# Hybrid decoder layer: activations read channel-major only, with rstd as a row, opening transfers in halves, and unread products ahead of the first matmul

## The chip, the cores and the metric

The kernel runs as one program on one core of a Trainium2 chip. The metric is the device time of one execution in microseconds. Three runs of the kernel before gave 767.24, 767.46 and 767.67 us, so the median is 767.46 us.

## The reference, cut to what matters

The layer has three token mixers in parallel, gated and merged, and then a mixture of experts. For the change only the opening matters: two RMS norms, and the projections that read them.

```python
def rmsnorm(x, g):
    y = x * rsqrt(mean(x * x, axis=-1, keepdims=True) + EPS)
    return y * g
h = rmsnorm(x, g_mix)                  # x (512 tokens, 1024 channels); all of w_in reads h
proj = h @ w_in
kv = rmsnorm(mem, g_mem) @ w_mem_kv    # mem (256 tokens, 1024 channels); k_m and v_m of the memory branch
k_m = rmsnorm(k_m, g_km)               # per head; v_m is used as it is
```

Everything is float32. The kernel keeps that precision in its projections by splitting each operand into a high part (a cast to fp32r) and a low part (the rest), and by adding three products: high by high, high by low and low by high.

## The kernel before

The work is written in program order, and a scheduler with a timing model of its own orders each engine's queue at build time. It prefers the earlier instruction among those it takes to be ready. Every queue is then executed in order. Two groups of instructions, the taps of the convolution and the top-k, are written with a low priority and fill what the vector engine (DVE) has left.

The opening is the section "mem kv". It multiplies the transposed memory tokens with w_mem_kv in eight chunks of 128 channels (`for k in range(KD)`). A chunk of weights is 128x1024 floats, 512 KB, from `raw_w` (L132) into a ring of three tiles. `split_w` makes its high part `wh` by a cast on ScalarE (ACT, L127) and its low part `wl` by a subtraction on DVE (L128), each in a ring of three as well. `evac_split` (L153 on ACT, L154 on DVE) does the same for an activation, times a gain per channel. Each chunk has 12 matmuls of 512 columns (`mm3`, L157 to L159) into four PSUM accumulators kv00, kv01, kv10 and kv11, first both halves of the columns for the memory tokens m=0, then for m=1. Three of the four have the PSUM tag "mm", which has three buffers.

Inside the same loop h is made. x is loaded with tokens on the partitions (four tiles of 512 KB), and a sum of squares per token (`sum_sq`, L223 on ACT, L225 on DVE) goes through `rsqrt` (L145 on DVE, then a power on GpSimd, L146). The tokens are scaled on DVE into `xn` (L265). 32 matmuls against an identity transpose them (L248), and eight `evac_split` make `hh` and `hl`. The raw memory tokens (two tiles of 512 KB) are loaded token-major as well, for their own sums of squares. They take two of the three buffers of the tag "hw", which three of the h tiles use.

What follows the opening is `cm_unit` (L314): 24 matmuls of 512 columns for 128 output channels, high by high over all eight chunks of h, then low weights by high h, then high weights by low h. The first one needs a PSUM buffer of the tag "mm", that is, one of the kv accumulators has to have been read. Such units, the attention branches and the gates run until about 415 us. There the pools of the first part are closed, and `fetch` (L779) starts to stream the 192 expert chunks of 512 KB through one queue, into buffers that the first part gives back. The queue of SyncE (SP) carries nearly all loads, in order.

Of the kernel before, what the change touches and what calls it, by code (L numbers as in the profile page):

```python
# [89 lines left out]
def build(nc, tc, I, O, dbg=None):  # L90
    V, A, G, T, SY = nc.vector, nc.scalar, nc.gpsimd, nc.tensor, nc.sync
    es = ExitStack()
    with es:
# [9 lines left out]
                dbg.mark(label)  # L103


        xt0 = [mpool.tile([P, D], F32, name=f"x{t}", tag="mg", bufs=4) for t in range(NT)]
        p1a, p1b, pps = ExitStack(), ExitStack(), ExitStack()
        hp = es.enter_context(tc.tile_pool(name="hp", bufs=1, side="right"))
        bp = p1b.enter_context(tc.tile_pool(name="bp", bufs=1, side="right"))
# [9 lines left out]
        tri16 = cpool.tile([P, 2 * P], BF16, name="tri16")  # L119
        nhalf = cpool.tile([P, 16], F32, name="nhalf")  # L120
        G.memset(nhalf, -0.5)

        def small(name, n, dt=F32, tag="small", bufs=16):
            return cpool.tile([P, n], dt, name=name, tag=tag, bufs=bufs)
# [53 lines left out]
        def g2(tag, name, dt=F32, shape=(P, 512)):  # L178
            pool = bp if tag in ("A", "B") else gp
            return pool.tile(list(shape), dt, name=name, tag=tag, bufs=BUFS[tag])  # L180

        def h_pairs(name):

            hi, lo = [], []
            for k in range(KD):
                if k >= 3:
                    x2 = hp.tile([P, 1024], F32R, name=f"{name}{k}", tag="hw" if k < 6 else "hx", bufs=3 if k < 6 else 2)
                    hi.append(x2[:, 0:512])
                    lo.append(x2[:, 512:1024])
# [27 lines left out]
            V.tensor_mul(t[:, :, 3, :], sin, g1)  # L217
            return t

        def sum_sq(ss, xt, on_act, tag="ms"):  # L220
            junk = g2(tag, "junk", BF16, (P, D))
            if on_act:
                A.activation(junk, xt, AF.Square, accum_out=ss)  # L223
            else:
                V.tensor_tensor_reduce(junk, xt, xt, scale=1.0, scalar=0.0, op0=ALU.mult, op1=ALU.add, accum_out=ss)  # L225


        mark("mem kv")
        kv_raw = [raw_w("kv", 0)]
        mx = [hp.tile([P, D], F32, name=f"m{i}", tag=("hx", "hw")[i // 2], bufs=2 + i // 2) for i in range(4)]  # L230
        SY.dma_start(mx[0], I["memt"][0])
        kv_raw.append(raw_w("kv", 1))
        SY.dma_start(mx[1], I["memt"][1])
        SY.dma_start(csg[:, 0:P], I["cst"][:, C_KEEP:C_KEEP + P])
        kv_raw.append(raw_w("kv", 2))
        mh = [g2("A", f"mh{k}", F32R) for k in range(4)]
        ml = [g2("A", f"ml{k}", F32R) for k in range(4)]
        for k in range(KD):
            o = (k % 2) * 256
            evac_split(mh[k // 2][:, o:o + 256], ml[k // 2][:, o:o + 256],  # L240
                       mx[k // 4][:, (k % 4) * 256:(k % 4 + 1) * 256], Q["g_mem"][:, k:k + 1])
        hh, hl = h_pairs("h")

        def transpose_x():
            for k in range(KD):
                ps = (trt if k % 2 == 0 else sct)()
                for t in range(NT):
                    T.transpose(ps[:, t * P:(t + 1) * P], xn[2 * t + k // 4][:, (k % 4) * P:(k % 4 + 1) * P], ident)  # L248
                evac_split(hh[k], hl[k], ps, Q["g_mix"][:, k:k + 1])

        kvp = [[mmt("kv00"), mmt("kv01")], [mmt("kv10"), pvt("kv11")]]
        xn, rm = [], []
        for k in range(KD):
            if k < NT:
                SY.dma_start(xt0[k], I["x"][k])
            elif k < NT + 2:
                SY.dma_start(mx[k - 2], I["mem"][k - NT])
            if k == 3:
                for t in range(NT):
                    ss = small("ss", 1)  # L260
                    sum_sq(ss, xt0[t], t != 1, "y")
                    rsqrt(ss, ss, 1.0 / D, EPS)
                    for i in range(2):
                        xn.append(g2("B", f"xn{t}{i}"))
                        V.tensor_scalar_mul(xn[-1], xt0[t][:, i * 512:(i + 1) * 512], ss)  # L265
            if k == 5:
                transpose_x()
            wh, wl = split_w(kv_raw[k] if k < RING else raw_w("kv", k))
            for m in range(2):
                o = (k % 2) * 256 + m * P  # L270
                ah, al = mh[k // 2][:, o:o + P], ml[k // 2][:, o:o + P]
                for n in range(2):
                    mm3(kvp[m][n], ah, al, wh[:, n * 512:(n + 1) * 512], wl[:, n * 512:(n + 1) * 512],
                        k == 0, k == KD - 1)
        SY.dma_start(sm[:, 2 * KD:], I["sm"][:, 2 * KD:])
        V.tensor_mul(gqk, Q["g_qm"], Q["g_km"])
        for m in range(2):
            rm.append(small("rm", 1, tag="rm", bufs=2))
            sum_sq(rm[m], mx[2 + m], True)
            rsqrt(rm[m], rm[m], 1.0 / D, EPS)  # L280
        vmh, vml, kn = [], [], []
        for m in range(2):
# [508 lines left out]
        def eat(tag, name, bufs=1, dt=F32):  # L791
            return ea.tile([P, 1024], dt, name=name, tag=tag, bufs=bufs)

        x_v = I["xt"].rearrange("k p n -> p k n")
        X = []
        for c in range(KD // 2):
            xt = rp.tile([P, 2, S], F32, name=f"xr{c}", tag="xc", bufs=2)
            SY.dma_start(xt, x_v[:, 2 * c:2 * c + 2])
            X.append(xt)
        wo_raw = [raw_w("wo", c) for c in range(KD)]  # L800
        gB = eat("wg", "gB")
# [504 lines left out]
def layout(x, mem, g_mix, w_in, b_gate, g_qa, g_ka, g_idx_k, conv_w, conv_b, ln_g, ln_b, g_mem, w_mem_kv,  # L1306
# [45 lines left out]
    def row(a):  # L1352
# [8 lines left out]
                 g_ffn=col(g_ffn, KD), b_r=np.concatenate([row(b_rg), row(b_re)], axis=1), w_r=wr, pad=np.zeros((P, 1), np.float32))  # L1361
    sm = np.ascontiguousarray(np.concatenate([parts[k] for k in S_OFF], axis=1).astype(np.float32))
    x, mem = f(x)[0], f(mem)[0]
    return dict(x=x.reshape(NT, P, D), xt=np.ascontiguousarray(x.T).reshape(KD, P, S), mem=mem.reshape(2, P, D),
                memt=np.ascontiguousarray(mem.T.reshape(2, 4, P, 256).transpose(0, 2, 1, 3)).reshape(2, P, D), wp=wp, we=we, sm=sm,
                gf=f(g_ffn), cst=constants())

# [34 lines left out]
```

## Time and profile before

| what | value |
|---|---|
| median of 3 runs | 767.46 us |
| profiled execution | 766.1 us |
| its span, first to last instruction | 764.2 us |
| mean granted TensorE clock | 0.991 |
| TensorE (PE) busy | 717.2 us, 94% |
| DVE busy | 477.5 us, 62% |
| ACT busy | 266.3 us, 35% |
| GpSimd (POOL) busy | 90.8 us, 12% |

The span is 1.9 us shorter than the profiled execution; the rest lies before the first and after the last instruction. Times in the trace count from the first instruction. PE is matmul, PEld the loading of its weights. A row of the timeline gives the start, the length, the engine, the line and what is written and read, and, in brackets, how long the engine had stood idle and what ended that. Matmuls are pipelined, so the distance between two starts tells more than the length of one. DMA share is the busy share of the core's 16 DMA engines.

### The profile page before, as it was taken

To read this page: it belongs to the slowest core of one execution; us is meant where nothing else is said; L and a number is where in the kernel's file an instruction comes from. 1 tells how busy PE (TensorE), PEld (TensorE's weight loads), DVE (VectorE), ACT (ScalarE), POOL (GpSimd) and SP (SyncE) were. 2 spreads that over 40 slices of the span, in tenths; PEclk is the share of its full clock that TensorE was granted. 3 is DMA by queue.
4 is the path that set the end of the run, shared out by engine and by line. 5 is a ranking of instruction groups with operands and counts; after the bars stand their busy time and mean duration, and the time that the engine had idled before them with its cause. 6 is when DMAs were issued, how large, how long until landed. Compare 5 with 4: busy or idle time off the path is not lost. (4 is left out here: it accounts for less than half of the span.)

```text
span 764.2 us, 10080 instructions
## 1 busy us (share of the span) xinstructions
PE 717.2 (94%) x3468; PEld 477.9 (63%) x3468; DVE 477.5 (62%) x1085; ACT 266.3 (35%) x503; POOL 90.8 (12%) x82
## 2 busy tenths in 40 slices
PE   6999999999999999999998999989999998889882
PEld 5778888887878778888776888834333333233220
DVE  5879989999999999999986844272112112111100
ACT  6722254455633376237775422101111111000100
POOL 1110010011000050000000000021226322100010
PEclk9999999999999999999999999999999999999997
DMA  9632221213222222321214799999999999999982
GB/s 357 232 121 82 88 79 55 82 58 111 83 83 83 83 84 72 98 80 55 84 55 150 273 378 340 329 315 377 400 378 359 354 370 387 361 381 395 391 324 49
DMA packets 56684, 161.13 MB, mean 211 GB/s; under 512 B 9508, under 2 KB 17956, under 8 KB 56624
## 3 DMA queue, kind: packets, MB, share of 16 engines
q1 hardware_dynamic: 42320, 147.74, 52.2%
q0 software_dynamic: 6624, 8.46, 4.8%
q10 hardware_dynamic: 7680, 4.20, 1.9%
q8 instruction: 29, 0.48, 0.2%
q14 instruction: 31, 0.25, 0.1%
HBM read 162.93 MB, written 13.11 MB: 230 GB/s over the span
## 5 line engine op out<-in xcount | busy, mean ns | idle before, releaser
L1165 PE MATMUL up<-we,xt 128*64 128x512 f32 x544 | 140.8, 599 | 5.4 <-DMA we<-in_we 5.4
L127 ACT CAST wh<-w 128x1024 fp32r<-128x1024 f32 (+2 forms) x75 | 78.3, 1046 | 80.4 <-PE proj L314 22.2
L128 DVE TENSOR_TENSOR wl<-w,wh 128x1024 fp32r<-128x1024 f32 (+2 forms) x75 | 90.9, 1213 | 13.0 <-ACT wh L127 11.2
L1165 PEld LDWEIGHTS up<-we,xt 128*64 128x64 f32 x544 | 39.1, 136 | 77.5 <-issue 59.1
L328 DVE SCALAR_TENSOR_TENSOR y<-u,conv_wh,y 128x512 f32<-128x512 f32 x120 | 84.2, 745 | 0.3
L1155 DVE COPY y<-dn 128x512 f32<-128x512 f32 x17 | 11.8, 692 | 108.9 <-PE dn L1179 108.9
L1179 PE MATMUL dn<-we,acth 128*64 128x512 f32 x272 | 73.5, 596 | 0.6 <-issue 0.6
L314 PE MATMUL gate<-h,wh 128*128 128x512 f32 x240 | 67.9, 397 | 0.0
L1154 ACT COPY y<-dn 128x512 f32<-128x512 f32 x17 | 10.0, 586 | 123.7 <-PE dn L1179 72.7
L1179 PEld LDWEIGHTS dn<-we,acth 128*64 128x64 f32 x272 | 24.0, 137 | 44.9 <-issue 36.3
L314 PEld LDWEIGHTS gate<-h,wh 128*128 128x128 f32 x240 | 44.4, 188 | 9.5
L1156 POOL DMA_INDIRECT out<-y,midx x16 | 25.4, 1585 | 147.5 <-DVE y L1155 106.5
L314 PE MATMUL gate<-h,wl 128*128 128x512 f32 x120 | 34.7, 399 | 0.0
L314 PE MATMUL mm<-h,wh 128*128 128x512 f32 x120 | 32.7, 397 | 0.0
L422 ACT ACTIVATE gt<-gate,bgate 128x512 f32<-128x512 f32 x24 | 16.5, 686 | 39.8 <-PE gate L314 39.5
L1138 ACT COPY xt<-xtr 128x512 f32<-128x512 f32 x18 | 10.4, 585 | 56.4 <-PE xtr L1137 52.4
L1173 DVE COPY acth<-atr 128x256 f32<-128x256 f32 x17 | 7.2, 425 | 36.0 <-PE atr L1171 28.4
L1148 DVE SCALAR_TENSOR_TENSOR acts<-up,mwt,acts 128x256 f32<-128x256 f32 x16 | 7.7, 484 | 32.3 <-ACT acts L1147 29.6
L604 DVE MAX8 v<-score 128x8 f32<-128x256 f32 (+2 forms) x48 | 26.6, 557 | 0.8
L605 DVE MATCH_REPLACE8 score<-v,score 128x256 f32<-128x256 f32 (+2 forms) x48 | 26.0, 542 | 0.0
L314 PEld LDWEIGHTS gate<-h,wl 128*128 128x128 f32 x120 | 22.4, 188 | 5.4 <-issue 0.5
L314 PEld LDWEIGHTS mm<-h,wh 128*128 128x128 f32 x120 | 22.4, 188 | 5.1
(400 smaller groups left out, 1442.0 us busy)
## 6 DMA issues: line engine op xcount, KB each, us to landing
we<-in_we SPq DMA_DIRECT2D x192, 512.0 KB
w<-in_wp SPq DMA_DIRECT2D x75, 512.0 KB
x<-in_x SPq DMA_DIRECT2D x4, 512.0 KB
xr<-in_xt SPq DMA_DIRECT2D x4, 512.0 KB
out<-x1t ACTq DMA_DIRECT2D x8, 256.0 KB
h2d<-x1t ACTq DMA_DIRECT2D x6, 256.0 KB
m<-in_memt SPq DMA_DIRECT2D x2, 512.0 KB
m<-in_mem SPq DMA_DIRECT2D x2, 512.0 KB
```

Of the source, the lines that this page charges most:

```text
L127: A.copy(wh, w)
L128: V.tensor_sub(wl, w, wh.bitcast(F32))
L314: T.matmul(ps, a[:, k * P:(k + 1) * P], b[k], start=(a is wh and b is rh and k == 0), stop=(b is rl and k == n - 1))
L328: V.scalar_tensor_tensor(Y[c], U[c][:, j:j + S], w, Y[c], op0=ALU.mult, op1=ALU.add)
L422: A.activation(t, ps, AF.Tanh, scale=0.5, bias=bgate[:, b * 8 + c:b * 8 + c + 1])
L604: V.max(v8, sel[t])
L605: V.match_replace(sel[t], v8, sel[t], GONE)
L1138: (A.copy if i or j == 0 else V.tensor_copy)(xt[i], ps.bitcast(F32))
L1155: V.tensor_copy(y[:, 512:1024], yp[1])
L1156: G.indirect_dma_start(out=O["out"], out_offset=bass.IndirectOffsetOnAxis(ap=ix[:, col:col + 1], axis=0), in_=y, in_offset=None, bounds_ch ...
L1165: T.matmul(ps[h * CAP:(h + 1) * CAP], xt[k // 4][:, o + h * CAP:o + (h + 1) * CAP], ws[h][:, i * 512:(i + 1) * 512], start=(k == 0), stop= ...
L1179: T.matmul(yp[n][h * CAP:(h + 1) * CAP], at[:, f * P + h * CAP:f * P + (h + 1) * CAP], ws[h][:, n * 512:(n + 1) * 512], start=(f == 0), st ...
```

## The change

- x is loaded only channel-major (`xt`, laid out by the host as four tiles of two chunks each), early in the opening. The token-major x, its sums of squares per token, the scaling into `xn` and the 32 transposes are gone.
- Squares are taken per channel on ACT, added up over the eight chunks in two accumulators, one on DVE and one on POOL. Eight matmuls against a column of ones sum over the channels (`rstd_x`), and `rsqrt` gives rstd. Four matmuls against the identity spread it as a row over all partitions (`norm_x`). Each chunk of x is multiplied by that row, even chunks on DVE (from PSUM), odd ones on POOL (from a copy in SBUF), and split into `hh` and `hl` by `evac_split`, now out of SBUF.
- Small copies out of `wl` of chunks 4 and 6 (`late`), overwritten at once, keep `rstd_x` and `norm_x` behind those splits.
- The first weight chunk and the first tile of memory tokens are loaded and the weights split in halves. Eight matmuls of 128 columns on a tile of ones, whose result nobody reads, stand ahead of the first real one.
- In each kv chunk the order of the four accumulators is by columns first, then by tokens. The raw memory tokens are loaded after the eight chunks, in four pieces, into the tag "B".

```diff
+        warm = cpool.tile([P, P], F32, name="warm")
+        V.memset(warm, 1.0)
...
+        junk = trt()
+        for _ in range(8):
+            T.matmul(junk[:, 0:P], warm, warm, start=True, stop=True)
+        w0 = wpool.tile([P, 1024], F32, name="w", tag="w")
+        mx = [hp.tile([P, D], F32, name=f"m{i}", tag="hx", bufs=2) for i in range(2)]
+        for i in range(2):
+            SY.dma_start(w0[:, i * 512:(i + 1) * 512], I["wp"][W_KEYS.index(("kv", 0)), :, i * 512:(i + 1) * 512])
+            SY.dma_start(mx[0][:, i * 512:(i + 1) * 512], I["memt"][0, :, i * 512:(i + 1) * 512])
+        kv_raw = [w0, raw_w("kv", 1)]
         SY.dma_start(mx[1], I["memt"][1])
-        SY.dma_start(csg[:, 0:P], I["cst"][:, C_KEEP:C_KEEP + P])
         kv_raw.append(raw_w("kv", 2))
+        x_v = I["xt"]
+        for c in range(2):
+            SY.dma_start(xt0[c], x_v[c])
...
-        def transpose_x():
+        xc = [xt0[k // 2][:, (k % 2) * 512:(k % 2 + 1) * 512] for k in range(KD)]
+        acc = [g2("y", f"acc{i}") for i in range(2)]
+        def squares(c):
+            for k in (2 * c, 2 * c + 1):
+                if c == 0:
+                    A.activation(acc[k], xc[k], AF.Square)
+                else:
+                    sq = g2("ms", "xsq")
+                    A.activation(sq, xc[k], AF.Square)
+                    (G if k % 2 else V).tensor_add(acc[k % 2], acc[k % 2], sq)
+        rx = small("rx", NT)
+        def rstd_x():
+            ss, one = trt(), small("one", 1)
+            V.tensor_copy(one, late[0][:, 0:1].bitcast(F32))
+            V.memset(one, 1.0)
+            for t in range(NT):
+                for i in range(2):
+                    T.matmul(ss[:, t:t + 1], acc[i][:, t * P:(t + 1) * P], one, start=(i == 0), stop=(i == 1))
+            rsqrt(rx, ss[:, 0:NT], 1.0 / D, EPS)
+        def norm_x():
+            row, rx2 = trt(), small("rx2", NT)
+            V.tensor_copy(rx2, late[1][:, 0:NT].bitcast(F32))
+            V.tensor_copy(rx2, rx)
+            for t in range(NT):
+                T.matmul(row[:, t * P:(t + 1) * P], rx2[:, t:t + 1].to_broadcast([P, P]), ident, start=True, stop=True)
+            rows = g2("ms", "row")
+            A.copy(rows, row)
             for k in range(KD):
-                ps = (trt if k % 2 == 0 else sct)()
-                for t in range(NT):
-                    T.transpose(ps[:, t * P:(t + 1) * P], xn[2 * t + k // 4][:, (k % 4) * P:(k % 4 + 1) * P], ident)
-                evac_split(hh[k], hl[k], ps, Q["g_mix"][:, k:k + 1])
+                if k % 2:
+                    G.tensor_mul(xc[k], xc[k], rows)
+                else:
+                    V.tensor_mul(xc[k], xc[k], row)
+                evac_split(hh[k], hl[k], xc[k], Q["g_mix"][:, k:k + 1])
...
         for k in range(KD):
...
             if k == 3:
+                kv_raw.append(raw_w("kv", 3))
+                for c in range(2, 4):
+                    SY.dma_start(xt0[c], x_v[c])
+                for c in range(4):
+                    squares(c)
+                SY.dma_start(csg[:, 0:P], I["cst"][:, C_KEEP:C_KEEP + P])
+            if k == 6:
+                rstd_x()
+            if k == 7:
+                norm_x()
...
-            for m in range(2):
-                for n in range(2):
+            for n in range(2):
+                for m in range(2):
...
+        mt = [g2("B", f"mt{i}") for i in range(4)]
+        for i in range(4):
+            SY.dma_start(mt[i], I["mem"][i // 2, :, (i % 2) * 512:(i % 2 + 1) * 512])
...
+            rh = small("rh", 2)
+            for i in range(2):
+                A.activation(g2("ms", "junk", BF16, (P, 512)), mt[2 * m + i], AF.Square, accum_out=rh[:, i:i + 1])
+            V.tensor_add(rm[m], rh[:, 0:1], rh[:, 1:2])
```

The later load of x for the residual reads the same new layout, in the same four transfers.

## Rows read from the trace of the kernel before

**Rows 1.** The page's 40 slices of the span: busy tenths.

```profile
PE   6999999999999999999998999989999998889882
DVE  5879989999999999999986844272112112111100
DMA  9632221213222222321214799999999999999982
```

**Rows 2.** Windows: start to end, length, busy us of each engine, clock, DMA share.

```profile
core 0: us, PE busy (x) PEld busy (x) DVE busy (x) ACT busy (x) POOL busy (x), PEclk, DMA share, GB/s
12.20:37.70 25.50, 23.94 (x117) 18.74 (x115) 21.31 (x45) 18.13 (x28) 3.32 (x6) 1.00 0.76 277
37.70:415.00 377.30, 373.11 (x1800) 302.05 (x1800) 354.04 (x804) 185.50 (x373) 26.88 (x15) 1.00 0.25 80
440.00:743.00 303.00, 285.58 (x1420) 132.29 (x1418) 75.36 (x196) 43.47 (x75) 55.80 (x48) 0.99 1.00 367
4.00:20.00 16.00, 12.86 (x48) 10.09 (x48) 10.94 (x24) 10.94 (x19) 2.25 (x4) 1.00 1.03 410
```

**Rows 3.** Timeline of SP where the expert chunks begin.

```profile
414.31 1.98 SPq L779 DMA_DIRECT2D we<-in_we  x4
```

**Rows 4.** Timeline of PE in the opening, and its end.

```profile
6.52 1.22 PE L157 MATMUL kv<-wh,mh 128*128 128x512 f32 x2 [6.52 <-ACT mh L153]
11.38 0.63 PE L159 MATMUL kv<-wh,ml 128*128 128x512 f32 x1
11.81 0.63 PE L157 MATMUL kv<-wh,mh 128*128 128x512 f32 x1
12.87 0.39 PE L157 MATMUL kv<-wh,mh 128*128 128x512 f32 x1
13.10 0.40 PE L158 MATMUL kv<-wl,mh 128*128 128x512 f32 x1
27.84 0.60 PE L248 MATMUL tr<-csg,xn 128*128 128x128 f32 x4
36.85 0.40 PE L159 MATMUL kv<-wh,ml 128*128 128x512 f32 x1
37.66 0.73 PE L314 MATMUL mm<-hh,wh 128*128 128x512 f32 x2 [0.41 <-DVE vml L154]
```

**Rows 5.** Timeline of ACT: loads that ended its idle time.

```profile
5.96 0.91 ACT L153 ACTIVATE mh<-m,sm 128x256 fp32r<-128x256 f32 x2 [0.29 <-DMA m<-in_memt]
7.18 1.05 ACT L127 CAST wh<-w 128x1024 fp32r<-128x1024 f32 x1 [0.32 <-DMA w<-in_wp]
16.45 1.05 ACT L127 CAST wh<-w 128x1024 fp32r<-128x1024 f32 x1 [0.21 <-DMA w<-in_wp]
```

**Rows 6.** Timeline of DVE, 20 to 25 us.

```profile
20.79 1.22 DVE L128 TENSOR_TENSOR wl<-w,wh 128x1024 fp32r<-128x1024 f32 x1
21.92 0.74 DVE L154 SCALAR_TENSOR_TENSOR hl<-tr,sm,hh 128x512 fp32r<-128x512 f32 x1
22.58 0.74 DVE L154 SCALAR_TENSOR_TENSOR hl<-sc,sm,hh 128x512 fp32r<-128x512 f32 x1
```

**Rows 7.** PE's records of fp32 matmuls later in the kernel, by tile: ns, first and last start.

```profile
L651 PE MATMUL rs<-identr,rc x8: 275/275/368, 290.7 to 291.6; 128*128 128x128 f32 x8
L646 PE MATMUL var<-cst,sq x8: 165/250/250, 288.4 to 289.1; 128*128 128x1 f32 x8
```

**Rows 8.** Elementwise work on 128x512 of the kinds that the change adds, by tile.

```profile
L654 DVE TENSOR_TENSOR y<-y,rs x4: 680/680/689, 291.9 to 293.7; 128x512 f32<-128x512 f32 x4
L642 ACT ACTIVATE sq<-y x3: 621/623/632, 283.9 to 285.7; 128x512 f32<-128x512 f32 x3
```

**Rows 9.** POOL's groups, by shape: busy us, mean ns of one, idle before.

```profile
L146 POOL TENSOR_TENSOR rsa<-rsa,nhalf 128x8 f32<-128x8 f32 x4 | 12.5, 3130 | 93.0 <-DVE rsa L145 93.0
L995 POOL MEMSET xg<- 128x1024 f32 x2 | 1.9, 956 | 60.3 <-PE tr L816 60.3
L146 POOL TENSOR_TENSOR rc<-rc,nhalf 128x4 f32<-128x4 f32 x1 | 1.0, 1008 | 8.4 <-DVE rc L145 8.4
```

More of the change, by code (lines that the diff above doesn't have):

```diff
@@ L103, in mark @@
                 dbg.mark(label)
-        xt0 = [mpool.tile([P, D], F32, name=f"x{t}", tag="mg", bufs=4) for t in range(NT)]
+        xt0 = [mpool.tile([P, D], F32, name=f"x{c}", tag="mg", bufs=4) for c in range(KD // 2)]
         p1a, p1b, pps = ExitStack(), ExitStack(), ExitStack()
@@ L218, in rope_tables @@
             return t
[L220 to L225, printed above, removed]
-        mark("mem kv")
[L229 to L232, printed above, removed]
+        mark("mem kv")
+        junk = trt()
[7 more added lines that the diff above has]
+        kv_raw = [w0, raw_w("kv", 1)]
         SY.dma_start(mx[1], I["memt"][1])
-        SY.dma_start(csg[:, 0:P], I["cst"][:, C_KEEP:C_KEEP + P])
         kv_raw.append(raw_w("kv", 2))
+        x_v = I["xt"]
+        for c in range(2):
+            SY.dma_start(xt0[c], x_v[c])
         mh = [g2("A", f"mh{k}", F32R) for k in range(4)]
@@ L251, in build @@
         kvp = [[mmt("kv00"), mmt("kv01")], [mmt("kv10"), pvt("kv11")]]
-        xn, rm = [], []
+        rm, late = [], []
         for k in range(KD):
[L254 to L257, printed above, removed]
             if k == 3:
[L259 to L268, printed above, removed]
-            for m in range(2):
-                o = (k % 2) * 256 + m * P
-                ah, al = mh[k // 2][:, o:o + P], ml[k // 2][:, o:o + P]
-                for n in range(2):
+                kv_raw.append(raw_w("kv", 3))
[8 more added lines that the diff above has]
+                norm_x()
+            if k == 0:
+                wh = spool.tile([P, 1024], F32R, name="wh", tag="wh")
+                wl = spool.tile([P, 1024], F32R, name="wl", tag="wl")
+                for i in range(2):
+                    split_into(wh[:, i * 512:(i + 1) * 512], wl[:, i * 512:(i + 1) * 512], w0[:, i * 512:(i + 1) * 512])
+            else:
+                wh, wl = split_w(kv_raw[k] if k < 4 else raw_w("kv", k))
+                if k in (4, 6):
+                    late.append(wl)
+            for n in range(2):
+                for m in range(2):
+                    o = (k % 2) * 256 + m * P
+                    ah, al = mh[k // 2][:, o:o + P], ml[k // 2][:, o:o + P]
@@ L278, in build @@
             rm.append(small("rm", 1, tag="rm", bufs=2))
-            sum_sq(rm[m], mx[2 + m], True)
+            rh = small("rh", 2)
+            for i in range(2):
+                A.activation(g2("ms", "junk", BF16, (P, 512)), mt[2 * m + i], AF.Square, accum_out=rh[:, i:i + 1])
+            V.tensor_add(rm[m], rh[:, 0:1], rh[:, 1:2])
             rsqrt(rm[m], rm[m], 1.0 / D, EPS)
@@ L792, in eat @@
             return ea.tile([P, 1024], dt, name=name, tag=tag, bufs=bufs)
-        x_v = I["xt"].rearrange("k p n -> p k n")
         X = []
@@ L797, in build @@
             xt = rp.tile([P, 2, S], F32, name=f"xr{c}", tag="xc", bufs=2)
-            SY.dma_start(xt, x_v[:, 2 * c:2 * c + 2])
+            SY.dma_start(xt.rearrange("p k n -> p (k n)"), x_v[c])
             X.append(xt)
@@ L1363, in layout @@
     x, mem = f(x)[0], f(mem)[0]
-    return dict(x=x.reshape(NT, P, D), xt=np.ascontiguousarray(x.T).reshape(KD, P, S), mem=mem.reshape(2, P, D),
+    return dict(xt=np.ascontiguousarray(x.T.reshape(KD // 2, 2, P, S).transpose(0, 2, 1, 3)).reshape(KD // 2, P, 2 * S), mem=mem.reshape(2, P, D),
                 memt=np.ascontiguousarray(mem.T.reshape(2, 4, P, 256).transpose(0, 2, 1, 3)).reshape(2, P, D), wp=wp, we=we, sm=sm,
```

## The prediction

> **What bounds the kernel now.** I read the slices of the page first, for where each engine is full; then the windows, for how full; then the timelines of the opening, for what each engine waits for; then groups by shape and tile, for prices. The slices show two regimes [rows 1]: PE at nine tenths almost throughout, and DMA light until slice 23 and full from there. The windows put numbers on it [rows 2]. From 37.7 to 415 us PE is busy 373.1 of 377.3 us, and from 440 to 743 us the DMA engines have a share of 1.00. The expert chunks that fill them are first issued at 414.31 [rows 3], into buffers that the first part gives back. So the chain is: the opening, then a PE queue with 4.2 us of idle time in it, then a DMA stream whose start hangs on that queue. What the opening saves up to the first `cm_unit` at 37.66 [rows 4] should come out at the end one for one, and what stays within the opening is lost. Only that instant is to be forecast.
>
> The opening itself shows three things. First, PE starts at 6.52, when the first piece of memory tokens has come (5.96 [rows 5]) and been cast. Its matmuls then start 0.43 us apart (11.38 to 11.81), and from 12.87 on 0.23 apart [rows 4]. 512 columns in 0.43 us is the 1.2 GHz level; 0.23 belongs to 2.4 GHz. The clock column of the windows reads 1.00 here and doesn't show it, so the distance of the starts is what I go by. Second, from 4 to 20 us the DMA engines are full, at 410 GB/s [rows 2], so 512 KB take 1.28 us. The fourth weight chunk comes only at 16.45 [rows 5], since four tiles of x went ahead of it. Third, from 12.2 to 37.7 PE is busy 23.9, DVE 21.3 and ACT 18.1 of 25.5 us [rows 2]: no engine has much to give.
>
> **The transfers.** The order in which they are issued sets the arrivals. The first weight chunk was due about 1.28 before the 5.96 of the memory tokens, 4.7; half of it comes 0.64 earlier, at 4.0, half of the tokens at 4.7, and both wholes at 6.0 as before. Then, 1.28 apart, come kv1 7.2, the second tokens 8.5, kv2 9.8, x0 11.0, x1 12.3, kv3 13.6 (before: 16.4), x2 14.9, x3 16.2, the identity (64 KB), kv4 17.7, kv5 19.0. The raw memory tokens move behind kv7.
>
> **Start and unread products.** The first matmul can start about 5.2 instead of 6.5. The unread products are fp32 matmuls of 128 columns; four such are eight records in 1.2 us at the high clock [rows 7], so eight are about 2 us, or 4 at 1.2 GHz: they fit before 5.2 and cost nothing. They are worth little, too. Chunk 4 can't be multiplied with its low part before 17.7 + 1.05 (cast [rows 5]) + 1.22 (subtraction [rows 6]) = 20.0. At the low clock until 12.2, from 5.2, 16 matmuls are done, and the 32 left of chunks 0 to 3 take 7.4 us at 0.23: 19.6. So even if the clock rose no earlier, PE would be there in time. I book 0 for halves and products; the gain of the opening comes from 20 us on.
>
> **PE from 20.0.** One matmul of chunk 4 is done by then, 47 remain: 47 x 0.23 = 10.8, to 30.8. The 32 transposes are gone: four of them take 0.60 with the last one's 0.27, so they start 0.11 apart [rows 4], 3.5 us less. New are eight matmuls of one column (four such are eight records that start within 0.7 us, 0.1 apart [rows 7]: 1.7 us for eight) and four for the row, 1.0 us. The kv matmuls end at 33.5 if none of these falls in a wait, at 31.8 if the eight do. Then a kv accumulator must be read. By the new order kv01 is complete three matmuls (0.7) before the end; ACT's evacuation of 128x512 (about the square's 0.62 [rows 8]) and DVE's subtraction, 0.74 [rows 6], follow. That is about 0.8 after the end: 32.6 to 34.3. Before, the end was about 37.2 and the first unit at 37.66.
>
> **DVE from 20.0.** `wl` of chunks 5 and 6 is done by about 22.6. rstd needs x3 squared (16.2 plus two times 0.62 [rows 8]), added, then `wl` of chunk 4 at 20.0, then the eight matmuls (21.8), the subtract-and-scale step, 0.2, the power on POOL, 1.0 [rows 9]: 23.1 with hand-overs. After a copy and the row matmuls it is 24.6 before the first chunk is multiplied. From there DVE has four multiplies at 0.68 (from PSUM, as with the row of the layer norm [rows 8]) = 2.7, eight subtractions 0.66 apart [rows 6] = 5.3, `wl` of chunk 7 1.2, the evacuation's subtraction 0.7, some 0.3 of small ones: 10.2, to 34.8. What it loses, eight scalings and one sum of squares, lay before that point. ACT has a similar load: casts of chunks 4 to 7 and the next unit's (5 x 1.05), eight evacuations, the row's copy, four half squares of the memory tokens at some 0.8, two reads of accumulators, 16 us from 17.7: 33.7. So three engines end within a microsecond of each other, and DVE is last.
>
> **POOL.** It gets three adds and four multiplies of two inputs on 128x512, which the trace doesn't show. Bounds: 0.48 each (half of a memset of 1024 columns, 0.956) and 3.13 (a power on eight columns) [rows 9]. I take 1.4: a memset moves one operand and these move three, and an add is nearer to that than to a power. The adds lie before 20 us, where DVE is idle for 5 of 16 us [rows 2]. The multiplies run from about 25.2 to 30.8, and the last h chunk is split by 32.3, inside DVE's 34.8. The Trainium skill, GPSIMD Engine Reference, section "Elementwise — side-by-side cycle accounting", has a float32 add of 2048 columns at 4497 ns on GpSimd, which gives an estimate of 1.1 us for 512; the sum would be the same by it.
>
> **The sum.** The first `cm_unit` starts at 34.8 instead of 37.66: 2.9 us less. The profiled execution was 766.1 us, so that would be 763.2; the median, 767.46, lies 1.4 above the profiled one, and becomes 764.6 us. What I book at nothing: the load order after 37 us (DMA share 0.25 there), the later load of x, the same bytes.
>
> **Rivals.**
>
> Larger gain. PE's bound holds alone, DVE fitting `wl` of chunk 7 and other work into its wait for rstd (22.6 to 24.6), and the eight small matmuls fall into the wait at 20: the first unit starts at 31.8 to 32.6, 5 to 6 us earlier: 762. For it: DVE is idle in that gap. Against it: the row reaches DVE only at 24.6, and eight chunks of h have to pass it.
>
> No change. `wl` of chunk 7 is written behind `norm_x` in the program. If DVE's queue has it behind all eight subtractions, at 24.6 + 8.0 + 1.2 = 33.8, eleven matmuls of chunk 7 come after it: 36.3, with the evacuation 37.1 to 37.3, a gain of 0.5: 767. For it: in the trace of before the `wl` of chunk 3 starts only at 20.79, though its cast was over at 17.5 [rows 5, 6]. Against it: the scheduler may use the gap.
>
> Slower. POOL's multiplies and DVE's subtractions keep each other out. DVE's subtraction now reads two operands from SBUF where it read one from PSUM. If every POOL multiply of length c stops DVE except during its own 2.7 us of multiplies from PSUM, DVE ends at 34.8 + 4c - 2.7: 37.7 at c = 1.4, the break-even, 40.1 at c = 2 (2.4 slower: 770), and more with the upper bound. So it decides above c = 1.4. Against it: no row of before has POOL and DVE compete on anything of this size. The Trainium skill states such a rule on the page SBUF — State Buffer, section "Who interferes with whom": a DVE instruction with two SBUF inputs and a GpSimd instruction that reads SBUF share an interface, and the second to issue waits for the whole of the first. Nothing in the trace of before tests that.
>
> That the halves and the unread products do nothing is part of the forecast. Without the cover of the wait at 20.0 they would be worth up to 1.3 us (start) plus 13 slow matmuls x 0.2 = 2.6.
>
> **How the numbers follow.** Forecast (1.5 to 5 us less, 762.5 to 766.0 by itself, likeliest 764.6) 0.52; larger gain 0.14; no change 0.18; slower 0.16. A measurement of this kernel can tell about 0.2%, 1.5 us, from no change. Faster by more: 0.52 + 0.14 = 0.66. Within: 0.18. Slower: 0.16. The range runs from a first unit at 31.6 (6 less, 761.5) to the first part of the slower case, 0.8 above the median of before (768.3); it leaves out the rest of the slower case and the tip of the larger gain, 2 in 10. A scheduler's new order further on could move either end by a microsecond; that lies in it.
>
> **What would show it.** First kv matmul at 5.0 to 5.5. The first `wl` matmul of chunk 4 at about 20.0 with a wait before it; if it comes much earlier the arrivals are wrong, and the halves and products were worth something. kv matmuls ending at 32 to 34; the first L314 matmul at 34.8 after a wait for DVE. POOL's multiplies at 1.4, with DVE's subtractions still 0.66 apart while they run; lengths over 1 us there speak for the slower rival. `wl` of chunk 7 in the gap or behind the subtractions tells the forecast from no change. The first expert chunk at 411.4, and the DMA share from there on unchanged. I am wrong if the first unit comes earlier and the first expert chunk doesn't, which would mean that DVE, at 354 of 377 us, and not PE paces the middle.

## The result, and the profile after

The changed kernel takes 778.31 us (median of 4 runs, 777.75 to 780.27) beside 767.57 for the kernel before: the ratio is 1.0137 (95% interval 1.0117 to 1.0156). It is slower by 10.7 us, where 2.9 less was forecast; the time lies 10 us above the range. The profiled execution took 778.38 us with a span of 776.6.

Windows of the kernel after, cut at the end of the kv matmuls, the first `cm_unit` and the first expert chunk (columns as in [rows 2]):

```profile
12.20:35.60 23.40, 21.82 (x103) 16.78 (x101) 14.59 (x27) 13.29 (x22) 7.60 (x6) 1.00 0.84 307
35.60:47.00 11.40, 0.00 (x0) 0.00 (x0) 10.91 (x19) 8.49 (x16) 6.31 (x5) 0.64 0.15 50
47.00:425.00 378.00, 374.85 (x1797) 303.12 (x1797) 354.12 (x806) 185.31 (x373) 26.66 (x15) 0.99 0.23 79
440.00:743.00 303.00, 287.42 (x1436) 139.27 (x1436) 85.60 (x211) 48.83 (x82) 56.75 (x50) 0.99 0.99 364
```

SP's timeline of the kernel after, where the expert chunks begin:

```profile
425.54 1.92 SPq L823 DMA_DIRECT2D we<-in_we  x4
```

The second window is the loss. For 11.4 us PE runs nothing while DVE is busy for 10.9 of them. The windows around it are much as before [rows 2]: PE full in the middle, the DMA engines full at 0.99 at the end. The first unit comes 9.3 us later (37.66 to 47.00), the first expert chunk 11.2 later (414.31 to 425.54 [rows 3]), the end of the span 12.4 later.

PE's timeline of the kernel after (L159 to L161 are the kv matmuls, L265 the columns that sum the squares, L274 the row of rstd, L358 `cm_unit`):

```profile
4.80 0.72 PE L159 MATMUL kv<-wh,mh 128*128 128x512 f32 x2
...
9.01 0.74 PE L159 MATMUL kv<-wh,mh 128*128 128x512 f32 x2 [2.56 <-ACT wh L129]
...
22.48 0.50 PE L160 MATMUL kv<-wl,mh 128*128 128x512 f32 x1 [0.57 <-DVE wl L130]
...
27.18 1.84 PE L265 MATMUL tr<-one,acc 128*128 128x1 f32 x16
...
31.73 1.06 PE L274 MATMUL tr<-csg,rx 128*128 128x128 f32 x8
...
35.15 0.40 PE L161 MATMUL kv<-wh,ml 128*128 128x512 f32 x1
47.00 1.65 PE L358 MATMUL mm<-hh,wh 128*128 128x512 f32 x3 [11.45 <-DVE vml L156]
```

The kv matmuls end at 35.55, 1.7 before those of the kernel before [rows 4]. What the transposes gave is there. But the columns run only at 27.18 and the row at 31.73, neither after a wait of PE: each stands in PE's queue behind a weight chunk's twelve matmuls (of chunk 5 and of chunk 6). Who needs them is seen on DVE (L255 adds squares, L130 is `wl`, L281 multiplies by the row, L156 splits h and the kv accumulator):

```profile
18.87 1.34 DVE L255 TENSOR_TENSOR acc<-acc,xsq 128x512 f32<-128x512 f32 x1 [0.37 <-ACT xsq L254]
20.70 1.72 DVE L130 TENSOR_TENSOR wl<-w,wh 128x1024 fp32r<-128x1024 f32 x1 [0.50 <-ACT wh L129]
22.46 0.15 DVE L261 COPY one<-wl 128x1 f32<-128x1 f32 x1
...
29.06 0.16 DVE L147 TENSOR_SCALAR rx<-tr 128x4 f32<-128x4 f32 x1 [3.88 <-PE tr L265]
...
33.45 1.88 DVE L281 TENSOR_TENSOR x<-x,tr 128x512 f32<-128x512 f32 x3 [0.88 <-ACT row L276]
35.29 4.64 DVE L156 SCALAR_TENSOR_TENSOR hl<-x,sm,hh 128x512 fp32r<-128x512 f32 x3
39.85 2.06 DVE L156 SCALAR_TENSOR_TENSOR h<-x,sm,h 128x512 fp32r<-128x512 f32 x3
...
42.44 0.22 DVE L323 TENSOR_TENSOR rm<-rh 128x1 f32<-128x1 f32 x2
...
43.17 1.21 DVE L130 TENSOR_TENSOR wl<-w,wh 128x1024 fp32r<-128x1024 f32 x1
...
46.20 0.75 DVE L156 SCALAR_TENSOR_TENSOR vml<-kv,rm,vmh 128x512 fp32r<-128x512 f32 x1 [0.49 <-ACT vmh L155]
```

DVE waits 3.88 us for the columns, and from the row at 33.45 it is busy almost without a pause until the accumulator is read at 46.20. The first three subtractions take 4.64 us, the next three of the same size 2.06. POOL says why (L279 are its multiplies, L148 the powers):

```profile
18.11 3.23 POOL L255 TENSOR_TENSOR acc<-acc,xsq 128x512 f32<-128x512 f32 x2 [1.64 <-ACT xsq L254]
29.30 1.04 POOL L148 TENSOR_TENSOR rx<-rx,nhalf 128x4 f32<-128x4 f32 x1 [7.96 <-DVE rx L271]
33.50 5.88 POOL L279 TENSOR_TENSOR x<-x,row 128x512 f32<-128x512 f32 x4 [3.15 <-ACT row L276]
42.93 2.53 POOL L148 TENSOR_TENSOR rm<-rm,nhalf 128x1 f32<-128x1 f32 x2 [3.55 <-DVE rm L147]
```

While POOL multiplies (33.50 to 39.38), a DVE subtraction takes 1.55 us; after that 0.69. Both engines pay: POOL's first two multiplies take 1.30 and 1.29 us, the last two, beside the subtractions, 1.72 and 1.71. The rms of the memory tokens is added only at 42.44, and POOL's powers on it run to 45.46, though no accumulator can be read without it: the evacuations multiply by it.

### The profile page after: what moved, and what is told of

Its sections match the earlier page's. It is cut to its first block, busy times and chain, and to the rows that moved or that the text cites. A ratio compares the mean times of both kernels' runs of the same rounds, so it can differ in the third digit from the quotient of the medians.

```text
span 776.6 us, 10113 instructions
## 1 busy us (share of the span) xinstructions
PE 722.2 (93%) x3476; PEld 481.3 (62%) x3476; DVE 481.9 (62%) x1087; ACT 268.9 (35%) x511; POOL 101.0 (13%) x86
## 5 line engine op out<-in xcount | busy, mean ns | idle before, releaser
L130 DVE TENSOR_TENSOR wl<-w,wh 128x1024 fp32r<-128x1024 f32 (+2 forms) x76 | 91.6, 1205 | 12.6 <-ACT wh L129 11.1
L358 PE MATMUL gate<-h,wh 128*128 128x512 f32 x240 | 67.9, 397 | 0.0
L358 PEld LDWEIGHTS gate<-h,wh 128*128 128x128 f32 x240 | 44.4, 188 | 9.5
L358 PE MATMUL gate<-h,wl 128*128 128x512 f32 x120 | 34.7, 399 | 0.0
L358 PE MATMUL mm<-h,wh 128*128 128x512 f32 x120 | 33.9, 406 | 0.0
L358 PEld LDWEIGHTS mm<-h,wh 128*128 128x128 f32 x120 | 23.0, 193 | 5.4
L358 PEld LDWEIGHTS gate<-h,wl 128*128 128x128 f32 x120 | 22.4, 188 | 5.4 <-issue 0.5
```

What stands on the lines that cost most here:

```text
L130: V.tensor_sub(wl, w, wh.bitcast(F32))
L358: T.matmul(ps, a[:, k * P:(k + 1) * P], b[k], start=(a is wh and b is rh and k == 0), stop=(b is rl and k == n - 1))
```

## The experiments

**Theory.** Three things lie one behind the other on DVE's queue: the row is late by its place in PE's queue; POOL's multiplies and DVE's subtractions keep each other waiting; the memory tokens' rms stands behind h. The halved transfers add a fourth, small loss. **Rivals:** PE's clock, which falls to 0.64 in the idle stretch; the opening's load order; a cost of per-channel normalization that no place in a queue removes.

Each row: ratio to the kernel before with its interval, then from the profiled execution the start of PE's first low-part matmul of weight chunk 4 (given for the kernel after and its edits up to 9), of the first `cm_unit` and of the first expert chunk (us). There is one profile of each kernel. In the kernel after and in edits 1, 3 and 4 nothing is changed up to chunk 4, and yet it starts anywhere between 21.76 and 22.48: the first loads land differently in each execution. So the price of an edit that acts behind chunk 4 is read best from chunk 4 to the first unit.

| kernel | ratio | chunk 4 | first unit | expert chunk |
|---|---|---|---|---|
| before | 1 | – | 37.66 | 414.31 |
| after | 1.0137 [1.0117, 1.0156] | 22.48 | 47.00 | 425.54 |
| 1 after + 44 unread products | 1.0115 [1.0090, 1.0140] | 21.78 | 46.38 | 425.24 |
| 2 after, POOL's multiplies out | 1.0069 [1.0042, 1.0096] | 22.83 | 43.55 | 421.52 |
| 3 after, row a chunk earlier | 1.0078 [1.0049, 1.0107] | 22.09 | 43.79 | 421.99 |
| 4 after, memory sums first | 1.0099 [1.0068, 1.0131] | 21.76 | 44.77 | 423.60 |
| 5 before + halves and products | 1.0018 [0.9999, 1.0037] | – | 38.50 | 415.15 |
| 6 after, no halves, no products | 1.0123 [1.0104, 1.0141] | 20.69 | 45.12 | 423.75 |
| 7 after, no halves | 1.0130 [1.0105, 1.0154] | 20.90 | 45.44 | 424.84 |
| 8 before, new load order | 0.9994 [0.9983, 1.0004] | – | 37.56 | 414.11 |
| 9 edits 2, 3, 4 and 7 together | 1.0038 [1.0023, 1.0053] | 21.09 | 38.01 | 417.24 |
| 10 new order, first try | 1.0064 [1.0043, 1.0084] | – | 42.42 | 419.08 |
| 11 new order, second | 1.0020 [0.9997, 1.0042] | – | 38.31 | 415.56 |
| 12 new order, third | 1.0003 [0.9990, 1.0017] | – | 37.37 | 415.05 |

**1. PE kept busy in the gap.** 44 unread products of 512 columns behind the last kv matmul.

```
+        for _ in range(44):
+            T.matmul(fill, mh[3][:, 0:P], wh[:, 0:512], start=True, stop=True)
```

> The changed kernel with 44 unread products of 512 columns behind the last kv matmul, about 10 of the 11.45 us in which PE waits there. Nothing else moves. If the wait cools the clock (the first unit's matmuls start 0.43 us apart until about 51 us), the unit runs at 0.23 from its start and the time falls by about 2.1 us, from 778.3 to 776.2. If the slow start of the unit has another cause, no change.

Measured 778.29 us. PE's timeline:

```profile
46.38 0.96 PE L361 MATMUL mm<-hh,wh 128*128 128x512 f32 x3 [1.47 <-DVE vml L156]
...
51.05 0.41 PE L348 MATMUL tr<-csg,kn 128*128 128x128 f32 x2 [2.08 <-DVE kn L340]
```

The unit's matmuls are now 0.23 apart (three in 0.96, where the kernel after took 1.65), and the time gained is lost in a wait of 2.08 us for the normalized keys. The first unit comes 0.62 earlier only because chunk 4 does (0.70). The first expert chunk starts 378.9 us after the first unit, in the kernel after 378.5. So the low clock was real, but it cost nothing that another wait would not have cost: it is no cause of the loss.

**2. Without POOL's multiplies.** The odd chunks of x are not scaled by rstd; all else stays.

```
-                if k % 2:
-                    G.tensor_mul(xc[k], xc[k], rows)
-                else:
+                if k % 2 == 0:
                     V.tensor_mul(xc[k], xc[k], row)
```

> The changed kernel without GpSimd's four multiplies: the odd chunks of x are left without rstd. Theory port (GpSimd's multiplies and DVE's subtractions keep each other out, and that is the loss): the time comes back to that of before or close, under 770. Theory late row (the row of rstd comes 9 us later than I had it, since its matmuls stand in PE's queue behind chunks 5 and 6, and everything behind it on DVE comes late with it): the exclusion is worth what three subtractions show, 4.64 instead of 2.0 us, so 2.7 us less, 775.6, with the first unit at about 44.3 instead of 47.0.

Measured 774.53 us. DVE's timeline:

```profile
35.65 2.08 DVE L156 SCALAR_TENSOR_TENSOR hl<-x,sm,hh 128x512 fp32r<-128x512 f32 x3
```

In the same timeline, 20 us earlier, is a subtraction for a chunk of h:

```profile
15.84 1.28 DVE L156 SCALAR_TENSOR_TENSOR h<-x,sm,h 128x512 fp32r<-128x512 f32 x1 [0.44 <-ACT h L155]
```

PE's timeline of the same kernel:

```profile
43.55 1.65 PE L356 MATMUL mm<-hh,wh 128*128 128x512 f32 x3 [7.65 <-DVE vml L156]
```

The three subtractions fall from 4.64 to 2.08 us: these 2.6 us are what the two engines cost each other. The first unit comes 3.45 earlier, more than that, because the edit does two more things. An odd chunk that nobody scales is ready early, so one subtraction (0.7) leaves the chain behind the row, and DVE no longer waits 0.49 for the accumulator's high part; against that, the row itself comes 0.35 later (33.80). So POOL's part is some three tenths of the loss, not the whole. The time lies between the two theories, 1.1 us from the 775.6 of the late row and over 4 above the 770 of the port.

**3. The row a chunk earlier.** `rstd_x` at chunk 5 and `norm_x` at chunk 6.

```
-            if k == 6:
+            if k == 5:
                 rstd_x()
-            if k == 7:
+            if k == 6:
                 norm_x()
...
-                if k in (4, 6):
+                if k in (4, 5):
```

> The changed kernel with the sum over channels written one chunk earlier (ahead of chunk 5) and the row and the multiplies too (ahead of chunk 6). Theory late row: the column matmuls start at about 24.5 instead of 27.2, the row at about 29 instead of 31.7, the first multiply at 30.5 instead of 33.45, and the first unit 2.9 us earlier, 44.1: 775.4. Theory port: the multiplies and subtractions only move together, PE's end of the kv matmuls and the wait behind it shift little, within 1 us of 778.3.

Measured 775.57 us. DVE's timeline:

```profile
30.32 1.88 DVE L281 TENSOR_TENSOR x<-x,tr 128x512 f32<-128x512 f32 x3 [1.76 <-ACT row L276]
32.17 4.68 DVE L156 SCALAR_TENSOR_TENSOR hl<-x,sm,hh 128x512 fp32r<-128x512 f32 x3
```

PE's timeline of the same kernel:

```profile
43.79 1.65 PE L358 MATMUL mm<-hh,wh 128*128 128x512 f32 x3 [8.62 <-DVE vml L156]
```

The first multiply moves by 3.13 us, the first unit by 3.21, the subtractions stay stretched. Chunk 4 was 0.39 earlier in this execution, so the edit itself is worth 2.8 us, about twelve matmuls at 0.23. What the two steps compute and read is the same; only their place in the queues differs, above all that of twelve small matmuls in PE's.

**4. The memory tokens' sums ahead of the row.** Their loads and squares move from behind the loop to chunk 6.

```
+            if k == 6:
+                mt = [g2("B", f"mt{i}") for i in range(4)]
...
+                    rsqrt(rm[m], rm[m], 1.0 / D, EPS)
                 rstd_x()
```

> The changed kernel with the load of the raw memory tokens and their sums of squares written ahead of the row of rstd (at chunk 6), nothing else moved. Theory memory sums (the kv accumulators can't be read because the addition of the memory tokens' squares stands on DVE behind eight chunks of h, at 42.44): the evacuation needs no sum any more, it runs at about 42.5 instead of 46.2, and the first unit starts 3 to 3.7 us earlier, at 43.3 to 44: 774.6 to 775.3. Theory port, or if h itself is what the first unit waits for: the unit may start earlier but stalls at its seventh matmul on the last h chunks, split at 43 to 44, and the time falls by under 1 us.

Measured 777.71 us. PE's timeline:

```profile
44.77 1.65 PE L358 MATMUL mm<-hh,wh 128*128 128x512 f32 x3 [7.74 <-DVE vml L156]
```

The first unit comes 2.23 earlier, although the row moved back from 33.45 to 34.97. Chunk 4 was 0.72 earlier here, so 1.5 us of it is the edit's. The 43.3 to 44 expected was not reached, and the time decides nothing: the median is 0.6 us less, as the other theory had it, and the ratio (interval to 1.0131) is hardly told from that of the kernel after. What speaks for the theory is that DVE reads the accumulator ahead of the last two chunks of h, and the path from the row to the first unit, 9.8 us instead of 13.55. That path also holds one piece of work less, the first conv weight's low part, which DVE now makes ahead of the row.

The row moved back because PE slowed down ahead of it. A window of the same kernel over eight kv matmuls (the clock stands third from the end):

```profile
29.69:33.20 3.51, 3.51 (x8) 2.78 (x9) 2.81 (x11) 0.26 (x1) 0.82 (x1) 0.51 0.57 155
```

At a granted clock of 0.51 they are 0.43 apart, which costs some 1.6 us. Edit 9 (0.52 from 26.2 to 29.7) and the third order (0.56 from 22.1 to 26.0) have such a stretch ahead of their rows too, and there as here the first unit came later than expected. By an estimate from the 0.2 us more that each of eight matmuls took, the three first units would else be at about 43.2, 36.5 and 35.9, close to what was expected of them; no run tests it.

**5 to 8. The start and the loads.** Halves and unread products alone on the kernel before; the kernel after without both; without the halves alone; and the kernel before with the fourth weight chunk loaded ahead of two tiles of x.

```
-        for i in range(2):
-            SY.dma_start(w0[:, i * 512:(i + 1) * 512], I["wp"][W_KEYS.index(("kv", 0)), :, i * 512:(i + 1) * 512])
-            SY.dma_start(mx[0][:, i * 512:(i + 1) * 512], I["memt"][0, :, i * 512:(i + 1) * 512])
...
+        SY.dma_start(mx[0], I["memt"][0])
```

> The kernel before with only the opening halves and the unread products of the change. My forecast booked these at nothing, since PE has to wait for a later weight chunk whichever way it starts: 767.5, within 1.5. Theory start counts: up to 1.3 (earlier first matmul) plus 2.6 (no slow matmuls) less, 763.6. Theory halves hurt: in the changed kernel the second half of the memory tokens came at 7.5 instead of 6.0 and PE waited 2.6 us for it; if that isn't covered here, 1.5 to 2.6 more, 769 to 770.

> The changed kernel without the halves and without the unread products, so that only the reading of x and the rstd row are new. Theory late row: the loss lies behind 20 us, PE reaches chunk 4 in time either way, 778.3 within 1. Theory halves hurt: the time falls by the wait of 2.6 or a good part of it, to 776 or lower. Theory start counts: it rises by up to 3.9.

> The changed kernel with the first weight chunk and the first memory tokens as whole transfers again, the unread products kept. If the halves are what cost the 1.6 us between the changed kernel and the one without halves and products, this gives 776.5 to 777 and a first unit at 45 to 45.5, like that one. If it was the products, it gives 778.3 and 47.0, like the changed kernel. If the products are worth something once the halves are gone (matmuls of the first chunks at 0.23 instead of 0.43 apart, up to 2.6 us), the first unit starts at 43 to 44.

> The kernel before with one thing taken from the changed one: the fourth weight chunk is loaded ahead of the last two tiles of x, and split ahead of the scalings. In before its low part was made only at 20.79 us. If PE's waits between 18 and 22 us are what the opening of before loses, the first unit starts 1 to 2 us earlier, 765.5 to 766.5. If the transposes then wait for x instead, which comes 1.3 us later, no change: 767.5.

Measured 768.47, 776.68, 777.55 and 767.06 us. The window of 4 to 6 us in the kernel after (DMA share and GB/s stand last):

```profile
4.00:6.00 2.00, 1.98 (x9) 1.55 (x9) 1.50 (x3) 1.04 (x3) 0.00 (x0) 1.00 0.83 258
```

The same window with whole transfers, the products kept:

```profile
4.00:6.00 2.00, 0.83 (x4) 0.53 (x3) 0.13 (x1) 1.04 (x1) 0.00 (x0) 1.00 1.03 402
```

With halves the first matmul starts at 4.80 instead of 6.70, but the second half of the memory tokens lands so late that PE then waits until 9.01. ACT's timeline of the kernel after shows what it waits for:

```profile
7.54 0.91 ACT L155 ACTIVATE mh<-m,sm 128x256 fp32r<-128x256 f32 x2 [2.40 <-DMA m<-in_memt]
```

The kernel before with the same start waits the same way, in PE's timeline:

```profile
8.77 0.73 PE L159 MATMUL kv<-wh,mh 128*128 128x512 f32 x2 [2.23 <-ACT wh L129]
```

Taking the halves out moves the first unit of the changed kernel by 1.56 us (47.00 to 45.44), and chunk 4 by as much (22.48 to 20.90); against the other executions with halves in edits 1, 3 and 4 chunk 4 moves by 0.9 to 1.2. Taking the products out as well gives 0.32 more. In the time neither kernel is told from the kernel after: their intervals overlap, and both times lie between their forecasts. Edit 5 stays within the 1.5 us of no change that was forecast. The new load order alone (edit 8) changes nothing, where 1 to 2 us less was one of the two forecasts.

**9. Four edits together.** Edits 2, 3, 4 and 7; again the odd chunks are not scaled.

> The four single edits of the changed kernel in one: whole first transfers, the sums for rstd and the row one weight chunk earlier, the memory tokens' sums ahead of them, and POOL's four multiplies left out (the odd chunks of x are not scaled by rstd). If the four costs add up (1.9, 3.2, 2.2 and 3.5 us of the first unit), the first unit starts at 36 to 37 and the time is 767 to 768.5, as before. If they hide one another, because PE's kv matmuls (end 35.55) and DVE's queue end close together, the first unit starts at 39 or later and the time is 770 or more; then the wait ahead of the first unit says which engine is late next.

Measured 769.74 us. PE's timeline:

```profile
38.01 0.97 PE L348 MATMUL mm<-hh,wh 128*128 128x512 f32 x3 [1.72 <-DVE vml L156]
...
42.48 1.05 PE L348 MATMUL mm<-hh,wl 128*128 128x512 f32 x3 [2.34 <-DVE wl L130]
```

Alone the four move the first unit by 3.45 + 3.21 + 2.23 + 1.56 = 10.45 us, or by 9.3 if edits 3 and 4 are counted from chunk 4; together by 8.99 of the 9.34 that were lost. So they add up, nearly, though not to the 36 to 37 that was expected: 38.01 lies between the two forecasts, and so does the time (the low clock ahead of the row, named under edit 4, is part of that). The first expert chunk is 2.93 behind that of before. The 2.34 us behind the first unit's start, for the first conv weight's low part, which DVE now reaches after h, and the 0.35 that the first unit is later are most of that.

**10 to 12. The scheme with another order, no work left out.** Whole transfers; adds and multiplies on DVE alone; the columns at chunk 4, the row at chunk 5; memory sums ahead; h's low parts deferred. The second try puts `wl` of chunks 5 and 6 ahead of the multiplies and the first conv weight ahead of the low parts; the third also `wl` of chunk 7 ahead of the last three multiplies, and reads the awaited accumulator ahead of the keys' squares.

```
+        def high_x(row, ks):
+            for k in ks:
+                V.tensor_mul(xc[k], xc[k], row)
+                A.activation(hh[k], xc[k], AF.Copy, scale=Q["g_mix"][:, k:k + 1])
+        def low_x():
+            for k in range(KD):
+                V.scalar_tensor_tensor(hl[k], xc[k], Q["g_mix"][:, k:k + 1], hh[k].bitcast(F32), op0=ALU.mult, op1=ALU.subtract)
```

> The changed kernel mended by the theory late row: whole first transfers, the sum over channels written ahead of chunk 4 and the row ahead of chunk 5, the memory tokens' sums ahead of the row, all adds and multiplies on DVE, and the eight subtractions that make the low parts of h behind the evacuation of the first kv accumulator. Late row and port together: the row reaches DVE at 25 to 27 us instead of 33.4, the high parts of h are there by 33, the first unit starts at 35.5 to 37.5, and the time is 765.5 to 768, at or a little under before. If instead the chain is bound by the sheer work on DVE and not by its start, the first unit stays above 40 and the time above 770.

> The scheme of the change with whole first transfers, the unread products kept, no work on POOL but its powers, the memory tokens' sums ahead of the row, and the row's matmuls in PE's queue behind the first four matmuls of chunk 5; unlike the previous version of this order, the subtractions for the weight chunks 5 and 6 stand ahead of the multiplies on DVE, and the eight low parts come behind the last weight chunk. If the loss is the sum of the late row, the exclusion by POOL and the late sums, as the single edits showed (3.2, 3.5 and 2.2 us of the first unit, and 1.9 for the halves), then the row is ready at about 25, the kv matmuls end at 34.5 to 35.5 without a wait of over 1 us for a weight chunk's low part, the first unit starts at 35.5 to 37, and the time is 765.5 to 768, within 0.2% of the kernel before or a little faster. If per-channel normalization has a cost of its own that these do not hold (DVE has eight multiplies of 512 columns in place of eight scalings that lay earlier), the first unit starts at 39 to 42 and the time is 770 to 772.

> The previous best order with two more moves: the low part of weight chunk 7 goes ahead of the last three of DVE's eight multiplies, and the accumulator that the first unit waits for is read ahead of the squares of the keys. In the run before, the low part cost PE 1.06 us of waiting and the accumulator's read 3.13 us ahead of the first unit at 38.31. If these two positions in the queues of DVE and ACT are all that is left, the kv matmuls end about 1 us earlier (34.2) and the first unit starts at 36.0 to 36.8, 1 to 1.6 us before that of the kernel before the change, and the time is 766 to 767.5, the same as before or 0.2% less. If a second reader is late (a chunk of h, which the multiplies give to ACT), the wait moves to that and the first unit stays at 38, the time at 768 to 769.5.

Measured 772.19, 769.52 and 767.73 us. DVE's timeline of the first try:

```profile
25.27 4.87 DVE L274 TENSOR_TENSOR x<-x,tr 128x512 f32<-128x512 f32 x8 [1.74 <-PE tr L272]
30.06 2.35 DVE L130 TENSOR_TENSOR wl<-w,wh 128x1024 fp32r<-128x1024 f32 x2
```

PE's timeline of the first try:

```profile
31.33 0.80 PE L160 MATMUL kv<-wl,mh 128*128 128x512 f32 x1 [5.17 <-DVE wl L130]
```

The row is there at 25.27, and the early row makes a new wait: two weight chunks' low parts stand behind eight multiplies, and PE waits 5.17 us. The first unit, at 42.42, and the time lie where the forecast for sheer work on DVE had them, but the next two tries do the same work in another order and lose less. PE's timeline of the second try:

```profile
33.05 0.50 PE L160 MATMUL kv<-wl,mh 128*128 128x512 f32 x1 [1.06 <-DVE wl L130]
...
38.31 0.96 PE L358 MATMUL mm<-hh,wh 128*128 128x512 f32 x3 [3.13 <-DVE vml L156]
```

And of the third:

```profile
37.37 0.97 PE L360 MATMUL mm<-hh,wh 128*128 128x512 f32 x3 [2.42 <-DVE vml L156]
```

With the queues in that order the whole loss is back: 1.0003 (0.9990 to 1.0017) beside before. Nothing beats the kernel before. All three tries missed their first forecast: the first by 4.9 us of the first unit, the second by 1.3, the third (36.0 to 36.8) by 0.6, since the wait for the accumulator stays at 2.42 us and the row, behind the stretch of low clock named under edit 4, comes only at 28.11.

## Why the prediction was wrong

**The step that failed** is in the part on DVE: "then the eight matmuls (21.8) ... After a copy and the row matmuls it is 24.6 before the first chunk is multiplied." Measured: 33.45, 8.85 us later. Of these, 2.7 are operands that came later (22.7 instead of 20.0), 5.6 are places in PE's queue (4.4 for the columns, 1.2 for the row), and the rest is about ACT's copy of the row (0.59), which ended DVE's wait at 33.45. The matmuls were timed from when their operands are ready, not from their place in PE's queue. Their operands were ready at about 22.7 (`one` copied at 22.46); they ran at 27.18, behind all that was written ahead of them, chunk 5's matmuls included, and ended at 29.0 instead of 21.8. The row went the same way behind chunk 6: its operand was there at about 30.55, and it ran at 31.73; from the columns' end to the first multiply it took 4.4 us, where I had 2.8. Edit 3 shows this: one chunk earlier in the queue, 3.1 us earlier on DVE, 2.7 of them by the edit. I had read "24.6" as a fact of the data and asked the question of queue order only of `wl` of chunk 7.

**The slower rival's mechanism came true**, on top. The prediction set it at 34.8 + 4c - 2.7 with c the POOL multiply. c was near: 1.47 measured in the mean (1.3 alone, 1.7 beside subtractions), 1.4 taken. By that rule it costs 3.2 us; the three stretched subtractions show 2.6. Alone it would by the rule have ended at 38.0, about where before was; I gave it 0.16 because no row of before could show it. With both corrections the old sum closes, 33.45 + 10.2 + 3.2 = 46.85 beside 47.00, but partly by luck: the exclusion came out 0.6 below the rule and the multiplies 0.3 below their 2.7, while small work took 0.4 more and a wait of 0.49 for the accumulator's high part was not in it. The 10.2 still holds one `wl`, now the first conv weight's at 43.17, since that of chunk 7 had gone ahead of the row. The rule of the Trainium skill, SBUF — State Buffer, section "Who interferes with whom", agrees with the trace: 1.55 us beside POOL's multiplies, 0.69 without, and the multiplies stretched as well.

**Mis-sized.** `wl` of chunk 4 was done at 22.4, not 20.0. Without halves PE waits for it until 20.90, so 1.6 of that is the halves: I had the whole of the memory tokens at 6.0 with or without them, and with them the second half came at about 7.5. So booking nothing for the halves was wrong: the early start is lost in the next wait, and they cost 0.9 to 1.6 us of chunk 4. `wl` also took 1.72 us instead of 1.23, partly beside a POOL add. The reading of the memory tokens' rms had no place in my chain; edit 4 prices it at 1.5 to 2.2 us. The estimate from the Trainium skill's GPSIMD Engine Reference, section "Elementwise — side-by-side cycle accounting", 1.1 us for a POOL add, is below all that the trace shows (1.31 us for the first add, 1.47 for the multiplies).

The kv matmuls end at 35.55, where 31.8 to 33.5 was forecast, mostly because chunk 4's first low-part matmul came 2.5 later (22.48).

**Right.** The transposes' gain on PE is there: the kv end moved from 37.25 to 35.55, and every bit of it went into waiting. The unread products were worth nothing, as booked (edits 6 and 7), and for the reason given: the time that they gain is lost again in waits for chunk 4, 0.50 and 0.71 us in edit 7 and none in edit 6. The first kv matmul came at 4.80 (5.2 forecast). What the first unit loses does arrive at the end, though not quite one for one: over all 14 profiles the first expert chunk starts 376.55 to 379.40 us after the first unit, 376.65 in the kernel before and 378.54 in the one after. The "no change" rival, `wl` of chunk 7 behind the subtractions, did not occur: it used the wait for the row.

**Open.** In the third order ACT reads the awaited accumulator only at 35.66, behind the last high parts of h, and DVE at 36.56, behind two low parts; the kv matmuls had ended at 34.95. Whether more reordering would beat before was not tried. Between the two profiled spans lie 12.4 us (10.7 between the medians): 9.3 up to the first unit, 1.9 from there to the first expert chunk, 1.2 behind it. The causes of the last two were not separated.

## What to carry to other kernels

A small matmul that other engines wait for costs little on PE and its whole queue place elsewhere: time it from what stands ahead of it in PE's order, not from its operands. When work moves off PE onto DVE, read which instruction every later reader on DVE now stands behind, since an early result can block as well as a late one (5.17 us in the tenth run). And work given to POOL isn't free for DVE when both read SBUF: count what a POOL multiply shares with such DVE work as DVE time (four of 1.47 us cost DVE 2.6 here). And where each kernel has one profile, count an edit's gain from the last point that both kernels reach by the same path: the landing of the first loads alone moved chunk 4 by up to 0.7 us here.

## What the runs showed of the hardware

Six executions with the first two transfers in halves (256 KB, 2 KB in each partition) moved 258 to 322 GB/s between 4 and 6 us; eight with whole ones, 395 to 426. In five of the six PE waited 0.9 to 2.6 us for the second half. Whether the size of the transfers or their order does it was not separated.

DVE and POOL on SBUF operands, by the length of the single records: a subtraction of 128x512 takes 0.74 to 0.75 us alone and 1.29 to 1.75 beside POOL's multiplies, an add 0.68 to 0.69 alone and 1.34 beside a POOL add. POOL's first two multiplies take 1.29 and 1.30 us, the two wholly beside subtractions 1.71 and 1.72.

In PE's idle stretch of 11.4 us the granted clock was 0.64, and the first unit's matmuls were 0.43 apart, the 1.2 GHz level, instead of 0.23; with unread products in the stretch (edit 1) they were 0.23 apart. The clock also fell while PE was at work: in edits 4 and 9 and in the third order to 0.51 to 0.56 for some 3.5 us, after the one-column matmuls, four matmuls of 512 columns and a wait of 0.35 to 0.37 us. In the first and second order the same sequence was followed by 1.00; what decides it is not shown.
